# Key parts stored row by row in turn, fewer transfers for queries and gate weights, a three-instruction root refinement and halved low-part subtractions in a two-layer fp32 encoder trunk

## Chip, cores and metric

The kernel runs on one core of one Trainium2 chip, as one launch. The metric is the device time of a run in microseconds (us); lower is better. The kernel before took 2789.21 us (median of three runs, 2776.15 to 2790.53). The engines are called PE (TensorE), DVE (VectorE), ACT (ScalarE), POOL (GpSimd) and SP (SyncE, which here only issues transfers).

## What is computed

Input and output are 2048 tokens of 1024 fp32 features. Layer 0 is a root-mean-square norm, one projection, two attention mixers side by side (A: a sliding window with two key heads for eight query heads, rotary embedding, attention sinks; B: eight heads over the token's own chunk and eight chunks before, with a relative bias), SiLU gates, an output projection and a residual add. Layer 1 has a norm, one projection, differential attention (C) over all earlier chunks, gates, an output projection and a residual add. Cut to what matters:

```python
def rms_norm(x, g):
    y = x * lax.rsqrt(jnp.mean(x * x, axis=-1, keepdims=True) + EPS)
    return y * g

def odd_layer(x, ...):
    h = rms_norm(x, norm_g)
    q, k, v, gate = jnp.split(h @ w_in, [C_QK, 2 * C_QK, 2 * C_QK + C_W], axis=-1)
    q1, q2 = (apply_rope(t, cos, sin) for t in parts(rms_norm(q, qn)))   # two 64-wide parts a head
    k1, k2 = (apply_rope(t, cos, sin) for t in parts(rms_norm(k, kn)))
    lam = exp(sum(lq1 * lk1)) - exp(sum(lq2 * lk2)) + lambda_init
    a = softmax(mask(q1 @ k1.T / 8)) - lam * softmax(mask(q2 @ k2.T / 8))
    o = rms_norm(a @ v, subln_g) * (1.0 - lambda_init)
    return x + (o * silu(gate)) @ w_out
```

## The kernel before, in words

The kernel is written in a tile language whose compiler pass allocates buffers, sets the semaphores and orders the instructions of each engine by a simulated timeline. The order in which the program traces its work is thus a priority and not the order on an engine; `issue_after(ins)` binds the instructions in its block to come behind `ins` on the same engine.

Nearly all products are taken at reduced precision in three passes: each operand is split into a high part (rounded by an ACT copy) and a low part (operand minus high part), and `mm3` (L211 to L216) multiplies high by high, high by low and low by high. So weights, hidden states, queries and keys exist as two tensors each, named H and L.

Four stages follow each other, with overlaps. The projection of layer 0 (`_project`, from 0 to about 600 us) and that of layer 1 (about 1090 to 1720 us) run over column groups of the weights and, within a group, over two blocks of 512 tokens, in two halves. `hidden` (L314) loads four x tiles of 128 tokens, takes the sum of squares on ACT, the inverse root in `rstd` (L196), scales the tile by root and gain on DVE (L325), transposes it on PE (L330) and splits it (L334 on ACT, L335 on DVE). `weights_by` (L298) loads two row blocks of 512 columns at a time and splits them: high part on ACT (L307), low part on POOL (L309), except four tiles of the very first group on DVE. A query or key group then has, for each 128 tokens, its sum of squares (L358, L359), its root in `rstd`, a scaling on DVE (L369), rotary products on DVE and POOL (L375 to L381), transposes (L388), and its split parts are stored to HBM by SP (L398, L399). `rstd` takes a first value y0 = exp(-0.5 ln(scale * ss + eps)) on ACT (L203, L204) and refines it by one Newton step in four DVE instructions (L205 to L208); the first of them does not read y0.

The mixers of layer 0 (`_mix0`, about 600 to 1090 us) and of layer 1 (`_mix1`, about 1720 to 2785 us) load queries and keys back from HBM, head by head. Scores need the query's high part against the key's high and low parts stacked on 128 partitions: 64 rows of high part, 64 rows of low part. So a key tile is filled by two transfers of 64 partitions (L591 and L592 in layer 0's `load_k`; L1104 and L1105 in layer 1's), and each query part is written twice into one tile, once for each half (L581 to L585; L937). In layer 1 an exponential (L969) follows each block of scores; DVE first takes the row maximum (L966). `combine` scales and adds the two softmaxes (L1001 on ACT, L1002 and L1003 on POOL); `values` transposes them on PE (L1017, into a PSUM pool `ptr` of two buffers), copies them on DVE (L1019) and multiplies by the values (L1021).

When a head's output is complete, `gate` copies it from PSUM and traces, two key tiles later, `rest` (L1053): the mean of squares as a product with ones on PE (L1056, into a buffer of the same pool `ptr`), its logarithm on ACT (L1057), a sum on DVE, an exponential on ACT (L1059), a product on DVE (L1060). The gates of layer 1 are projected beside the attention (`gates`, L1153): their split weights come from HBM in pieces of four row blocks, high and low part by one transfer each (L1165). The output projection of layer 1 fetches finished heads back (`fetch`, L1092), splits them on ACT and POOL (L1082, L1083), and runs on PE as `com`.

SP issues nearly all transfers from one in-order queue; each takes it about 0.3 to 0.6 us, and an issue that waits for a buffer holds up all behind it.

Of the kernel before, what the change touches and what calls it, by code (L numbers as in the profile page):

```python
# [18 lines left out]
P = 128  # L19
# [67 lines left out]
class Trunk:  # L87
# [15 lines left out]
    def scratch(self):  # L103
        dram = self.ctx.enter_context(self.tc.tile_pool(name="scr", bufs=1, space=DRAM))

        def d(name, shape):
            return dram.tile(shape, F32, tag=name, name=name)

        self.s0 = {
            "aqH": d("aqH", [4, P, S]), "aqL": d("aqL", [4, P, S]),  # L110
            "akH": d("akH", [1, P, S]), "akL": d("akL", [1, P, S]),
            "av": d("av", [S, 2 * 192]),
            "bqH": d("bqH", [4, P, S]), "bqL": d("bqL", [4, P, S]),
            "bkH": d("bkH", [4, P, S]), "bkL": d("bkL", [4, P, S]),
# [5 lines left out]
            "qH": d("qH", [8, P, S]), "qL": d("qL", [8, P, S]),  # L120
            "kH": d("kH", [8, P, S]), "kL": d("kL", [8, P, S]),
# [4 lines left out]
            "wgH": d("wgH", [8, P, KT, P]), "wgL": d("wgL", [8, P, KT, P]),  # L126
# [69 lines left out]
    def rstd(self, pool, ss, n, scale, tag):  # L196
# [5 lines left out]
        ln, y0, ms, u, r = t("ln"), t("y0"), t("ms"), t("u"), t("r")  # L202
        nc.scalar.activation(ln, ss, AF.Ln, bias=self.eps, scale=scale)  # L203
        nc.scalar.activation(y0, ln, AF.Exp, scale=-0.5)  # L204
        nc.vector.tensor_scalar(ms, ss, scale, EPS, ALU.mult, ALU.add)  # L205
        nc.vector.scalar_tensor_tensor(u, y0, -0.5, y0, ALU.mult, ALU.mult)
        nc.vector.tensor_tensor(u, u, ms, ALU.mult)
# [16 lines left out]
    def _project(self, es, layer):  # L224
# [35 lines left out]

        g_in = xp.tile([P, D], F32, tag="g_in", name=n + "g_in", bufs=1)
# [36 lines left out]
        def weights_by(c0, width, W, wH, wL, first=False):  # L298
            for kh in range(4):
# [5 lines left out]
                for k in range(2):  # L305
                    h, l = weight_tiles()
                    nc.scalar.activation(h[:, :width], ws[:, k, :width], AF.Copy)  # L307
                    low = nc.vector if first and k else nc.gpsimd
                    low.tensor_tensor(l[:, :width], ws[:, k, :width], f32(h[:, :width]), ALU.subtract)  # L309
                    wH.append(h)  # L310
                    wL.append(l)
                yield

        def hidden(b, i, between=()):  # L314
            hH, hL = hidden_tile("H", i), hidden_tile("L", i)
            between = iter(between)
            for j in range(NTB):
                t = b * NTB + j
                xt = xp.tile([P, D], F32, tag="xt", name=n + "xt")
                nc.sync.dma_start(xt, x[t * P:(t + 1) * P, :])  # L320
# [4 lines left out]
                nc.vector.scalar_tensor_tensor(xt, xt, r, g_in, ALU.mult, ALU.mult)  # L325
# [58 lines left out]
        def pairs_out(xs, npair, b, o):  # L384
            for p in range(npair):
# [12 lines left out]
                nc.sync.dma_start(s[o["dH"]][o["p0"] + p, :, b * BLK:(b + 1) * BLK], f32(eH))  # L398
                nc.sync.dma_start(s[o["dL"]][o["p0"] + p, :, b * BLK:(b + 1) * BLK], f32(eL))  # L399
# [9 lines left out]
        def put_gate(s, i, k, part, w):  # L409
            nc.sync.dma_start(  # L410
                s["wg" + part][4 * i:4 * i + 4, :, k, :].rearrange("c p d -> p c d"), w.rearrange("p (c d) -> p c d", c=4)
# [20 lines left out]
        for half in range(2):  # L432
# [4 lines left out]
            if half == 0 and layer == 0:  # L437
# [3 lines left out]
                h = [hidden(blocks[0], 0, by)]  # L441
# [111 lines left out]
    def _mix0(self, es):  # L553
# [22 lines left out]
        def load_q(H, L, h, b, res):  # L576
# [4 lines left out]
            nc.sync.dma_start(f32(qd[0:HD, :]), s[H][h // 2, r, tok])  # L581
            nc.sync.dma_start(f32(qd[HD:P, :]), s[H][h // 2, r, tok])
            ql = ld.tile([P, BLK], F32R, tag="ql", name=n + "ql", bufs=3)
            nc.sync.dma_start(f32(ql[0:HD, :]), s[L][h // 2, r, tok])
            self.asked = nc.sync.dma_start(f32(ql[HD:P, :]), s[L][h // 2, r, tok]).ins  # L585
            res["q"] = (qd, ql)

        def load_k(ks, H, L, p, row, k0, k1):
# [21 lines left out]
        def load_group(b, g):  # L610
# [3 lines left out]
            load_k(ks, "akH", "akL", 0, g, k0, k1)  # L614
# [114 lines left out]
        def scores_b(h, b, res):  # L729
            k0, k1 = max(0, (b - 1) * BLK), (b + 1) * BLK  # L730
            load_q("bqH", "bqL", h, b, res)
            ks = load_k(ld.tile([P, 1024], F32R, tag="ks", name=n + "ks"), "bkH", "bkL", h // 2, h % 2, k0, k1)
# [171 lines left out]
    def _mix1(self, es):  # L904
# [25 lines left out]
        def load_q(h, b):  # L930
            tok = slice(b * BLK, (b + 1) * BLK)
            qd = ld.tile([P, 2, BLK], F32R, tag="qd", name=n + "qd")
            ql = ld.tile([P, 2, BLK], F32R, tag="ql", name=n + "ql")
            for part, q in (("qH", qd), ("qL", ql)):
                both = s[part][h, :, tok].rearrange("(m r) t -> r m t", m=2)
                for o in range(2):
                    nc.sync.dma_start(f32(q[o * HD:(o + 1) * HD]), both)  # L937
# [103 lines left out]
        def gate(h, b, O, g):  # L1041
# [11 lines left out]
            def rest():  # L1053
# [3 lines left out]
                nc.scalar.activation(sq, ms, AF.Ln, bias=self.eps, scale=1.0 / P)  # L1057
# [16 lines left out]
        def y_tiles(h, b):  # L1074
# [3 lines left out]
            return [pl.tile([P, BLK], F32R, tag=t, name=n + "y" + t, bufs=3 if pl is ld else None) for t in tags]  # L1078
# [296 lines left out]
```

## Time and profile before

| | us | share of the span |
|---|---|---|
| profiled execution | 2787.15 | |
| its span | 2785.3 | |
| PE busy | 2684.9 | 96% |
| PE weight loads (beside PE) | 2162.2 | 78% |
| DVE busy | 1815.7 | 65% |
| ACT busy | 1594.9 | 57% |
| POOL busy | 1412.4 | 51% |

The granted PE clock is 0.994 of full speed on average. The transfers of the SP and ACT queues take 61.9% of the time of the 16 DMA engines, 518.50 MB in all.

In the rows that follow, a line of the waits names the engine and source line, the instruction that it waited for, and then us in total, times and longest. A line of the time-ordered view gives start, duration, engine, line, operation, output<-inputs, shape and count; in brackets the idle time before it and what ended it. Names are those of tiles, with a letter or two ahead for the stage (p0 and p1: projections, m: mixers of layer 0, c: mixer of layer 1).

### The profile page before, as it was taken

The page shows a single profiled execution, that of the slowest core. Times are in us where ns is not written, and L with a number is a line of the kernel's source. Part 1 is how long each engine was busy: PE and PEld are TensorE (multiplying, and loading weights), DVE is VectorE, ACT ScalarE, POOL GpSimd, SP SyncE. Part 2 cuts the span into 40 slices and gives each one's busy share as a digit, 9 for nine tenths or more (in the row PEclk, how much of TensorE's full clock was granted, in tenths as well). Part 3 has the DMA queues.
Part 4 walks back from the last instruction along what each step waited for, and adds up shares of the span by engine and source line. Part 5 has one row for each costly group of instructions (what it writes and reads, how often), then busy time and mean ns, then how long its engine had stood idle before and what let it go on. Part 6 is the DMA issues. An engine that isn't in the chain of part 4 may idle for free.

```text
span 2785.3 us, 43597 instructions
## 1 busy us (share of the span) xinstructions
PE 2684.9 (96%) x13384; PEld 2162.2 (78%) x13384; DVE 1815.7 (65%) x4520; ACT 1594.9 (57%) x3975; POOL 1412.4 (51%) x1471
## 2 busy tenths in 40 slices
PE   7999999999899999999999999999999999999999
PEld 5888887888788888788887888777777776676776
DVE  7762286337777777447833783478887777776762
ACT  5443544358767676333343333588887776676771
POOL 3641254245435344336453652467775666667661
PEclk9999999999999999999999999999999999999999
DMA  5674348569787766744494436899877766465542
GB/s 173 226 241 146 110 131 274 189 180 242 203 217 180 185 186 194 218 167 129 143 291 164 144 122 211 249 243 244 212 218 206 198 183 188 121 185 145 166 127 93
DMA packets 350585, 518.50 MB, mean 186 GB/s; under 512 B 42384, under 2 KB 134288, under 8 KB 350352
## 3 DMA queue, kind: packets, MB, share of 16 engines
q1 hardware_dynamic: 345744, 507.32, 61.9%
q10 hardware_dynamic: 4608, 8.39, 0.8%
q8 instruction: 107, 1.75, 0.3%
q14 instruction: 126, 1.03, 0.1%
HBM read 358.56 MB, written 157.02 MB: 185 GB/s over the span
## 4 chain that ended last, share of the span: by engine, by line
PE 69%; DMA 5%; DVE 4%; ACT 3%; issue 1%; POOL 1%; SPq 0%; ACTq 0%; DVEq 0%; POOLq 0%
PE cO L1021 7%; PE p1mm L214 6%; PE p1mm L215 6%; PE p1mm L216 6%; PE cS L962 4%; PE cS L963 4%; PE ctr L1017 3%; PE mom L214 2%; PE mom L216 2%; PE mom L215 2%; PE mtrB L782 2%; PE com L214 2%; PE com L216 2%; PE com L215 2%; PE cG L214 2%; PE cG L215 2%
## 5 line engine op out<-in xcount | busy, mean ns | idle before, releaser
L969 ACT ACTIVATE cP<-cS,cnm 128x512 f32<-128x512 f32 (+3 forms) x640 | 394.6, 623 | 148.9 <-DVE cnm L966 132.6
L966 DVE TENSOR_REDUCE cnm<-cS 128x1 f32<-128x512 f32 (+3 forms) x640 | 373.7, 601 | 55.1 <-PE cS L963 48.7
L1003 POOL TENSOR_TENSOR cP<-cP,cP 128x512 f32<-128x512 f32 (+1 forms) x320 | 357.3, 1144 | 19.0 <-ACT cP L1001 18.6
L1002 POOL TENSOR_SCALAR cP<-cP,crl,cel 128x512 f32<-128x512 f32 (+3 forms) x288 | 208.4, 736 | 261.5 <-DVE crl L984 126.3
L309 POOL TENSOR_TENSOR p0wL<-p0ws,p0wH 128x512 fp32r<-128x512 f32 (+1 forms) x140 | 169.8, 1238 | 279.2 <-ACT p0wH L307 261.3
L214 PE MATMUL p1mm<-p1wH,p1hH 128*128 128x512 f32 x768 | 300.7, 393 | 0.8 <-ACT p1hH L334 0.8
L216 PE MATMUL p1mm<-p1wH,p1hL 128*128 128x512 f32 x768 | 300.2, 391 | 0.0
L215 PE MATMUL p1mm<-p1wL,p1hH 128*128 128x512 f32 x768 | 299.5, 390 | 0.0
L1021 PE MATMUL cO<-cpt,cv 128*128 128x512 f32 (+3 forms) x640 | 285.5, 531 | 9.1 <-DVE cpt L1019 9.0
L962 PE MATMUL cS<-ck,cqd 128*128 128x512 f32 (+3 forms) x640 | 261.7, 413 | 11.6 <-ACT cP L969 10.3
L1019 DVE COPY cpt<-ctr 128x512 f32<-128x512 f32 (+1 forms) x320 | 190.7, 605 | 101.7 <-PE ctr L1017 98.8
L214 PE MATMUL p0mm<-p0wH,p0hH 128*128 128x512 f32 (+1 forms) x640 | 238.0, 375 | 6.9 <-ACT p0vt L497 5.0
L216 PE MATMUL p0mm<-p0wH,p0hL 128*128 128x512 f32 (+1 forms) x640 | 238.9, 374 | 1.6 <-DVE p0hL L335 1.6
L215 PE MATMUL p0mm<-p0wL,p0hH 128*128 128x512 f32 (+1 forms) x640 | 239.1, 374 | 0.0
L963 PE MATMUL cS<-ck,cql 128*128 128x512 f32 (+3 forms) x640 | 234.0, 370 | 1.4 <-DMA cql<-qL 1.4
L1017 PEld LDWEIGHTS ctr<-ident,cP 128*128 128x128 f32 x1088 | 136.8, 141 | 119.4 <-issue 62.6
L309 POOL TENSOR_TENSOR p1wL<-p1ws,p1wH 128x512 fp32r<-128x512 f32 x112 | 152.3, 1383 | 134.2 <-ACT p1wH L307 129.4
L1001 ACT ACTIVATE cP<-cP,cc 128x512 f32<-128x512 f32 (+1 forms) x320 | 189.0, 653 | 16.4 <-DVE cc L987 15.4
L1017 PE MATMUL ctr<-ident,cP 128*128 128x128 f32 x1088 | 174.4, 273 | 5.7 <-POOL cP L1003 5.7
L214 PEld LDWEIGHTS p1mm<-p1wH,p1hH 128*128 128x128 f32 x768 | 144.6, 188 | 29.8 <-ACT p1hH L334 1.2
L216 PEld LDWEIGHTS p1mm<-p1wH,p1hL 128*128 128x128 f32 x768 | 144.3, 188 | 29.7
L767 POOL TENSOR_SCALAR mPB<-mPB,mbr 128x640 f32<-128x640 f32 (+4 forms) x128 | 92.5, 735 | 147.6 <-DVE mbr L764 89.6
(320 smaller groups left out, 6972.9 us busy)
## 6 DMA issues: line engine op xcount, KB each, us to landing
p1ws<-in_od_w_in_dram SPq DMA_DIRECT2D x56, 512.0 KB, 3.7
p0ws<-in_ev_w_in_dram SPq DMA_DIRECT2D x48, 512.0 KB, 4.6
ck<-kH SPq DMA_DIRECT2D x144, 128.0 KB, 3.8
ck<-kL SPq DMA_DIRECT2D x144, 128.0 KB, 3.9
cv<-v SPq DMA_DIRECT2D x72, 256.0 KB, 4.6
cqd<-qH SPq DMA_DIRECT2D x64, 256.0 KB, 6.5
cql<-qL SPq DMA_DIRECT2D x64, 256.0 KB, 7.8
cwH<-wgH SPq DMA_DIRECT2D x64, 256.0 KB, 5.5
```

Source lines behind the costliest of these rows:

```text
L214: mm(ps, aH, bH, start=first, stop=False)
L215: mm(ps, aH, bL, start=False, stop=False)
L216: mm(ps, aL, bH, start=False, stop=last)
L309: low.tensor_tensor(l[:, :width], ws[:, k, :width], f32(h[:, :width]), ALU.subtract)
L962: mm(ps, qd[:, m, js], kt[:, :wd], start=True, stop=False)
L963: self.anchor = mm(ps, ql[:, m, js], kt[:, :wd], start=False, stop=True).ins
L966: nc.vector.tensor_reduce(nm[:, m, z:z + 1], ps, AX.X, ALU.max, negate=True)
L969: exp = nc.scalar.activation(chunks[z][:, :wd], ps, AF.Exp, bias=nm[:, m, z:z + 1], accum_out=acc).ins
L1002: nc.gpsimd.tensor_scalar(p1, p1, rl[:, 0:1], e1, ALU.mult, ALU.mult)
L1003: nc.gpsimd.tensor_tensor(p1, p1, p2, ALU.add)
L1017: nc.tensor.transpose(turned[:, (j - j0) * P:(j - j0 + 1) * P], us[j][kt // 4][:, kk:kk + P], self.ident)
L1021: mm(O[:, j0 * P:], v, T[:, :wd], start=(kt == 0), stop=(kt == nkt - 1), skip_group_check=True)
```

## The change

Seven things are changed.

1. Keys: high and low parts lie in one HBM tensor, `[pairs, 128, 2, 2048]`, so that row r's high part is followed by its low part. A key tile is then loaded by one transfer of 128 partitions, whose partition 2r + i holds part i of row r. The stores of the projections write every other 8 KB row of this tensor.
2. Queries: the doubled query is loaded with one transfer for each part, each row read twice into neighbouring partitions. In layer 1 the HBM tensor becomes `[8, 64, 4, 2, 512]`, so that one row of one block is 4 KB in one piece; a query store of layer 1's projection becomes two transfers of 64 partitions.
3. Gate weights of layer 1: high and low part in one HBM tensor and one SBUF tile, one transfer where there were two.
4. `rstd`: three DVE instructions behind y0 instead of one ahead and three behind.
5. The first x tile of layer 0 is loaded ahead of the gain, and its scaling is done in two halves of 512 columns.
6. The low parts of the weights in layer 0 are subtracted in two halves of 256 columns (layer 1 keeps one instruction).
7. In `rest`, the logarithm is bound to come behind the latest exponential of the scores (`self.exp`) on ACT.

The diff, cut to its core:

```diff
@@ scratch
+        ak, bk, ck = d("ak", [1, P, 2, S]), d("bk", [4, P, 2, S]), d("ck", [8, P, 2, S])
...
-            "qH": d("qH", [8, P, S]), "qL": d("qL", [8, P, S]),
-            "kH": d("kH", [8, P, S]), "kL": d("kL", [8, P, S]),
+            "qH": d("qH", [8, HD, NB, 2, BLK]), "qL": d("qL", [8, HD, NB, 2, BLK]),
+            "k": ck, "kH": ck[:, :, 0], "kL": ck[:, :, 1],
...
-            "wgH": d("wgH", [8, P, KT, P]), "wgL": d("wgL", [8, P, KT, P]),
+            "wg": d("wg", [8, P, 2, KT, P]),
@@ rstd
-        nc.vector.tensor_scalar(ms, ss, scale, EPS, ALU.mult, ALU.add)
-        nc.vector.scalar_tensor_tensor(u, y0, -0.5, y0, ALU.mult, ALU.mult)
-        nc.vector.tensor_tensor(u, u, ms, ALU.mult)
+        nc.vector.scalar_tensor_tensor(u, ss, EPS / scale, y0, ALU.add, ALU.mult)
+        nc.vector.scalar_tensor_tensor(u, u, -0.5 * scale, y0, ALU.mult, ALU.mult)
         nc.vector.scalar_tensor_tensor(r, u, 1.5, y0, ALU.add, ALU.mult)
@@ _project
+        early = load_x((NB - 1) * NTB) if layer == 0 else None
         g_in = xp.tile([P, D], F32, tag="g_in", name=n + "g_in", bufs=1)
...
-                    low.tensor_tensor(l[:, :width], ws[:, k, :width], f32(h[:, :width]), ALU.subtract)
+                    step = width // 2 if layer == 0 and width == 512 else width
+                    for c in range(0, width, step):
+                        cs = slice(c, c + step)
+                        low.tensor_tensor(l[:, cs], ws[:, k, cs], f32(h[:, cs]), ALU.subtract)
...
-                nc.vector.scalar_tensor_tensor(xt, xt, r, g_in, ALU.mult, ALU.mult)
+                step = 512 if first else D
+                for c in range(0, D, step):
+                    cs = slice(c, c + step)
+                    nc.vector.scalar_tensor_tensor(xt[:, cs], xt[:, cs], r, g_in[:, cs], ALU.mult, ALU.mult)
...
-                nc.sync.dma_start(s[o["dH"]][o["p0"] + p, :, b * BLK:(b + 1) * BLK], f32(eH))
-                nc.sync.dma_start(s[o["dL"]][o["p0"] + p, :, b * BLK:(b + 1) * BLK], f32(eL))
+                for part, t in (o["dH"], eH), (o["dL"], eL):
+                    to = s[part][o["p0"] + p]
+                    if layer == 0 or o["tab"] == "k":
+                        nc.sync.dma_start(to[:, b * BLK:(b + 1) * BLK], f32(t))
+                        continue
+                    for m in range(2):
+                        nc.sync.dma_start(to[:, b, m], f32(t[m * HD:(m + 1) * HD]))
@@ _mix0
+            for q, part in (qd, H), (ql, L):
+                twice = s[part][h // 2, r, tok].unsqueeze(1).to_broadcast([HD, 2, BLK])
+                self.asked = nc.sync.dma_start(f32(q), twice).ins
...
-            nc.sync.dma_start(f32(ks[0:HD, :k1 - k0]), s[H][p, r, k0:k1])
-            nc.sync.dma_start(f32(ks[HD:P, :k1 - k0]), s[L][p, r, k0:k1])
+            nc.sync.dma_start(f32(ks[:, :k1 - k0]), s[K][p, r, :, k0:k1].rearrange("r i t -> (r i) t"))
@@ _mix1
-                both = s[part][h, :, tok].rearrange("(m r) t -> r m t", m=2)
-                for o in range(2):
-                    nc.sync.dma_start(f32(q[o * HD:(o + 1) * HD]), both)
+                twice = s[part][h, :, b].rearrange("r m t -> r (m t)").unsqueeze(1).to_broadcast([HD, 2, 2 * BLK])
+                nc.sync.dma_start(f32(q).rearrange("p m t -> p (m t)"), twice)
...
-                nc.scalar.activation(sq, ms, AF.Ln, bias=self.eps, scale=1.0 / P)
+                with tc.issue_after(self.exp):
+                    nc.scalar.activation(sq, ms, AF.Ln, bias=self.eps, scale=1.0 / P)
...
-            nc.sync.dma_start(f32(k[r, :]), s["kH"][h, r, tok])
-            self.loaded = nc.sync.dma_start(f32(k[o, :]), s["kL"][h, r, tok]).ins
+            rows = s["k"][h, m * HD:(m + 1) * HD, :, tok].rearrange("r i t -> (r i) t")
+            self.loaded = nc.sync.dma_start(f32(k), rows).ins
...
-                            for part in "HL":
-                                t = ld.tile([P, 4, P], F32R, tag="w" + part, name=n + "w" + part, bufs=3)
-                                self.loaded = nc.sync.dma_start(f32(t), s["wg" + part][c, :, k:k + 4, :]).ins
+                            w = ld.tile([P, 2, 4, P], F32R, tag="w", name=n + "w", bufs=3)
+                            self.loaded = nc.sync.dma_start(f32(w), s["wg"][c, :, :, k:k + 4, :]).ins
```

More of the change, by code (lines that the diff above doesn't have):

```diff
@@ L259, in weight_tiles, with load_x @@
                     yield self.yt.tile([P, 512], F32R, tag="yt", name=n + "w" + part)
+        def load_x(t):
+            xt = xp.tile([P, D], F32, tag="xt", name=n + "xt")
+            nc.sync.dma_start(xt, x[t * P:(t + 1) * P, :])
+            return xt
+        early = load_x((NB - 1) * NTB) if layer == 0 else None
         g_in = xp.tile([P, D], F32, tag="g_in", name=n + "g_in", bufs=1)
@@ L318, in hidden @@
                 t = b * NTB + j
-                xt = xp.tile([P, D], F32, tag="xt", name=n + "xt")
-                nc.sync.dma_start(xt, x[t * P:(t + 1) * P, :])
+                first = early is not None and j == 0
+                xt = early if first else load_x(t)
                 junk = xp.tile([P, D], F32, tag="vb", name=n + "junk", bufs=2 - layer)
@@ L410, in put_gate @@
             nc.sync.dma_start(
-                s["wg" + part][4 * i:4 * i + 4, :, k, :].rearrange("c p d -> p c d"), w.rearrange("p (c d) -> p c d", c=4)
+                s["wg"][4 * i:4 * i + 4, :, "HL".index(part), k, :].rearrange("c p d -> p c d"),
+                w.rearrange("p (c d) -> p c d", c=4),
             )
@@ L440, in _project @@
                 next(by)
-                h = [hidden(blocks[0], 0, by)]
+                h = [hidden(blocks[0], 0, by, early)]
             else:
@@ L731, in scores_b @@
             load_q("bqH", "bqL", h, b, res)
-            ks = load_k(ld.tile([P, 1024], F32R, tag="ks", name=n + "ks"), "bkH", "bkL", h // 2, h % 2, k0, k1)
+            ks = load_k(ld.tile([P, 1024], F32R, tag="ks", name=n + "ks"), "bk", h // 2, h % 2, k0, k1)
             vt = lv.tile([P, 8, P], F32R, tag="v", name=n + "vB")
@@ L930, in load_q @@
         def load_q(h, b):
-            tok = slice(b * BLK, (b + 1) * BLK)
             qd = ld.tile([P, 2, BLK], F32R, tag="qd", name=n + "qd")
@@ L1077, in y_tiles @@
             pl, tags = place[h, b]
-            return [pl.tile([P, BLK], F32R, tag=t, name=n + "y" + t, bufs=3 if pl is ld else None) for t in tags]
+            if pl is ld:
+                t = ld.tile([P, 2, BLK], F32R, tag="w", name=n + "yw", bufs=3)
+                return t[:, 0, :], t[:, 1, :]
+            return [pl.tile([P, BLK], F32R, tag=t, name=n + "y" + t) for t in tags]
         def split(h, b, o):
@@ L1139, in _mix1 @@
         ended = set()
-        place = {(h, NB - 1): (ld, ("wH", "wL")) if h < 3 else (kp, ("k0", "k1")) for h in (0, 1, 2, 6, 7)}
+        place = {(h, NB - 1): (ld, None) if h < 3 else (kp, ("k0", "k1")) for h in (0, 1, 2, 6, 7)}
         def load_w(c, k, to):
```

21 lines of the change are left out of this document (7 added, 14 removed).

## The prediction

> **What bounds the kernel now.** I read the engine shares on the page first, then what TensorE (PE) waits for, then the windows table, then time-ordered rows around the longest waits.
>
> ```profile
> span 2785.3 us, 43597 instructions
> ...
> PE 2684.9 (96%) x13384; PEld 2162.2 (78%) x13384; DVE 1815.7 (65%) x4520; ACT 1594.9 (57%) x3975; POOL 1412.4 (51%) x1471
> ...
> L969 ACT ACTIVATE cP<-cS,cnm 128x512 f32<-128x512 f32 (+3 forms) x640 | 394.6, 623 | 148.9 <-DVE cnm L966 132.6
> ```
>
> TensorE is busy 96% of the span, and the change touches none of its matmuls. So all that can be won lies in its idle time, 2785.3 - 2684.9 = 100.4 us, and in time that it runs at a reduced clock. The profiled execution took 2787.15 us, 1.85 us more than its span; the median of the three runs is 2789.21 us (2776.15 to 2790.53). I work out a difference against the profiled execution and take it off the median. Of this kernel a measurement can tell about 0.5%, 14 us, from no change.
>
> What PE waits for (engine and line, releaser: us in total, times, longest):
>
> ```profile
> PE p0trh L330 <- DVE p0xt L325: 13.4, 3, 12.7
> PE cS L962 <- ACT cP L969: 10.3, 9, 4.1
> ...
> PE cG L214 <- DMA cwH<-wgH: 5.2, 3, 4.3
> PE p0mm L214 <- ACT p0vt L497: 5.0, 4, 2.3
> ...
> PE p0trq L388 <- DVE p0xn L369: 2.1, 1, 2.1
> PE mSB L626 <- DMA mql<-bqL: 2.1, 1, 2.1
> PE cS L963 <- DMA cql<-qL: 1.4, 3, 0.7
> ```
>
> The idle time is many short waits with different releasers; no single one is worth 14 us. The windows show where they lie, and a second cost behind them (stretch and length; busy time of each engine; granted PE clock, DMA share, GB/s):
>
> ```profile
> 0.00:70.00 70.00, 51.83 (x243) 41.99 (x244) 55.40 (x127) 36.05 (x85) 23.43 (x24) 0.98 0.56 174
> 420.00:490.00 70.00, 66.92 (x309) 54.86 (x308) 42.98 (x96) 32.07 (x78) 32.31 (x31) 0.98 0.83 276
> 1400.00:1470.00 70.00, 67.41 (x333) 55.99 (x331) 27.24 (x46) 35.19 (x70) 36.57 (x28) 1.00 0.95 308
> 1540.00:1610.00 70.00, 70.00 (x334) 58.47 (x333) 56.62 (x87) 22.96 (x47) 44.15 (x34) 1.00 0.40 125
> 1750.00:1820.00 70.00, 65.68 (x295) 51.44 (x296) 32.73 (x115) 39.40 (x105) 29.60 (x35) 0.95 0.86 254
> 1890.00:1960.00 70.00, 67.96 (x332) 51.17 (x331) 61.82 (x196) 62.65 (x174) 52.45 (x60) 1.00 0.99 247
> ```
>
> Where PE stalls for more than about 2 us, the granted clock of the window falls too: 0.95 of 70 us is 3.5 us lost on top of the wait, 0.98 is 1.4. In layer 1's projection (1540 to 1610) PE is busy all 70.00 us: nothing can be won there, and added work on other engines costs nothing.
>
> **The change, part by part.**
>
> *The start.* The first x tile goes ahead of the gain, and its scaling is cut in two.
>
> ```profile
> 0.73 0.38 SPq L262 DMA_DIRECT2D p0g_in<-in_ev_norm_dram  x1
> 1.17 0.42 SPq L301 DMA_DIRECT2D p0ws<-in_ev_w_in_dram  x1
> 1.64 0.46 SPq L320 DMA_DIRECT2D p0xt<-in_x_dram  x1
> ...
> 18.62 1.15 ACT L307 ACTIVATE p0wH<-p0ws 128x512 fp32r<-128x512 f32 x2 [1.72 <-DMA p0ws<-in_ev_w_in_dram]
> ```
>
> PE's first transposes wait 12.7 us. With x as the first of three 512 KB transfers instead of the third, and half a scaling ahead of them, they can begin up to some 5 us sooner. But the first output tile sums over all eight row blocks of the weights, and the last two are converted at 18.62 us, after a transfer whose place in the queue the change leaves alone. So most of the lead is given back there. I take -2 us, bounds -5 and +1 (the first weights are now third in line).
>
> *Low parts in halves, and the root in three.* The 128x512 subtractions of layer 0 on POOL become two of 128x256. Rows of DVE, of POOL, and durations by line (ns min/median/max):
>
> ```profile
> 462.72 1.22 DVE L207 TENSOR_TENSOR p0q8u<-p0q8u,p0q8ms 128x8 f32<-128x8 f32 x1
> 463.98 1.19 DVE L208 SCALAR_TENSOR_TENSOR p0q8r<-p0q8u,p0q8y 128x8 f32<-128x8 f32 x1
> ```
> ```profile
> 461.37 5.00 POOL L309 TENSOR_TENSOR p0wL<-p0ws,p0wH 128x512 fp32r<-128x512 f32 x4 [9.44 <-ACT p0wH L307]
> ```
> ```profile
> L309 POOL TENSOR_TENSOR p0wL<-p0ws,p0wH x140: 723/1290/1485, 7.3 to 600.2; 128x512 fp32r<-128x512 f32 x124, 128x256 fp32r<-128x256 f32 x16
> ```
> ```profile
> L205 DVE TENSOR_SCALAR p0q8ms<-p0qss x48: 160/172/1256, 35.1 to 515.7; 128x8 f32<-128x8 f32 x48
> ```
> ```profile
> 2357.12 2.62 DVE L980 TENSOR_TENSOR cbelow<-cnm,ctop 128x8 f32<-128x8 f32 x1
> ```
>
> A DVE instruction on 128x8 takes 0.17 us as a rule and 1.2 here. POOL's four run 1.25 us each, so they end at 462.62, 463.87, 465.12; the two DVE instructions end at 463.94 and 465.17, each just behind one. So DVE is held to the end of POOL's instruction, and three dependent ones take three of them, 3.75 us. The smallest form, 0.72 us, must be the 256-wide one, so the hold falls to 3 x 0.72 = 2.2, 1.5 less. The trace charges PE with 2.1 us for the wait behind this chain (L388), and with 5.0 for four behind L497, which copies the tiles that the same kind of chain scales; the longest is 2.3. Taking 1.5 off the 2.1, 1.5 off the 2.3 and 1.0 off the other three, with the 1.4 of reduced clock in 420 to 490, gives -5 us. POOL's price, 124 x (2 x 0.72 - 1.29) = 19 us, is covered where POOL is busy for 32 of 70 us; uncovered it is what the rotated tiles queue behind, 1 to 2 us. Bounds -7 and +2.
>
> The Trainium skill, SBUF — State Buffer, section "SBUF: two separate sides", says that POOL and DVE share a pair of ports, locked for the whole instruction by whoever starts first. The rows above agree; by that rule POOL's second half may also start first, and L980 above, which sat through more than one POOL instruction, shows that this happens. Then the part is worth nothing; it counts in the second case below.
>
> The root refinement drops L205: 128 calls by the code (80 in layer 0, 48 in layer 1) x 0.17 = 22 us of DVE. The dropped instruction did not depend on the root's first value; three dependent ones stay behind that. So -1 us, bounds -3 and 0.
>
> *Fewer transfers.* A key load goes from two DMAs of 64 partitions to one of 128, a query from four to two, a gate weight from two to one. SP's queue, ACT, and the issues (KB each, median us to landing):
>
> ```profile
> 2558.96 0.60 SPq L937 DMA_DIRECT2D cql<-qL  x1
> 2559.67 0.54 SPq L1092 DMA_DIRECT2D coy<-o  x1
> ```
> ```profile
> 2567.98 0.63 ACT L1082 ACTIVATE cy<-coy 128x512 fp32r<-128x512 f32 x1 [4.18 <-DMA coy<-o]
> ```
> ```profile
> ck<-kL SPq DMA_DIRECT2D x144, 128.0 KB, 3.9
> cv<-v SPq DMA_DIRECT2D x72, 256.0 KB, 4.6
> cqd<-qH SPq DMA_DIRECT2D x64, 256.0 KB, 6.5
> ...
> qH<-p1eH SPq DMA_DIRECT2D x32, 256.0 KB, 2.8
> ```
>
> A transfer of 256 KB by 64 partitions lands in 6.5 us, one by 128 in 4.6. Where half-height loads prevail (1890 to 1960) the DMA engines move 247 GB/s at a share of 0.99, in the window at 1400 308 at 0.95: 249 against 324 for a full share. I take that ratio, 0.77, for the backlog. In the rows above a fetch queued behind queries was issued at 2559.67 and used at 2567.98, 8.3 us later; ACT stood still for 4.18 us with exponentials behind it, and PE waited 4.1 (the longest of cS <- ACT). A backlog shorter by 0.23 x 8.3 = 1.9 us takes 1.9 off this wait, 1.9 off the query wait of 2.1, 2.8 off the three gate-weight waits (4.3 to 2.4, the short ones to nothing) and 1.4 off L963: 8.0. Of the reduced clock behind these (3.5 in 1750 to 1820, where the gate weights' wait lies, and by estimate a 0.98 window's 1.4 behind each of the other two long ones, 6.3 in all), I let a third go with them, 2 us. So -10 us; bounds 0 (same bytes, same time) and -19 (all of 12.8 us of waits and of 6.3 of clock).
>
> The Trainium skill, SBUF — State Buffer, section "Door 1: The DMA port swizzle", holds that 64 adjacent partitions reach half of the ports. By that rule alone half-height loads take double time, and this part would be near its -19. The trace's ratio is 0.77, not 0.5, and I keep to it.
>
> In return each query store in layer 1's projection becomes two of 64 partitions: 64 more issues by 0.6 us, 38 us of SP there, and some transfer time on a DMA share of 0.40. PE has no idle time to lose to it in that stage, its weights being loaded ahead. 0 us; 3 if the cover goes.
>
> *The logarithm behind the exponential (L1057).*
>
> ```profile
> ACT csq L1057 <- PE cms L1056: 42.9, 12, 10.9
> ```
>
> ACT stands still 42.9 us in twelve places of 32 (8 heads x 4 blocks) because the logarithm is queued ahead of exponentials whose inputs are there, and waits for a product that PE reaches later. Tied behind the latest exponential, it waits little. Most of ACT's idle time is covered: of the 10.3 us of cS <- ACT, 4.1 is the fetch above, and 6.2 are left for this and all else. I take half, -3, bounds -6 and a loss, below.
>
> The sum: -2 - 5 - 1 - 10 + 0 - 3 = -21 us, 2787.15 to 2766 in the profiled frame, 2768 us as a median. The ends add to -40 and, without the loss below, to +6.
>
> **The rivals.**
>
> *Waits move and nothing is seen.* The same bytes cross the same 16 engines, so landings hardly improve; POOL's second half starts before DVE gets in; an earlier start is eaten by later weights. Then the start gives 1 to 2, the root 1, the logarithm 3: 2789 - 6 = 2783 us. For it: DMA waits are only 10 of 100 us of PE's idle time, and the order of instructions on all engines is laid out anew, so other short waits can appear. Against it: the ratio 0.77, and a hold that ends with each POOL instruction.
>
> *Slower: the logarithm holds a PSUM buffer.* Its input, the mean of squares, lies in one of only two buffers that PE also transposes into. Behind an exponential that itself waits for DVE's maximum (132.6 us of such waits in the row of L969), the logarithm frees that buffer later, and PE has one left for transposes. If each of the 32 is later by two exponentials of 0.62 us and PE has nothing else, that is +40 us; with 18 us of other gains, 2789 + 22 = 2811 us. It decides from 1 us each (32 us, less 18, is 14). For it: twenty of the 32 show no wait today, so they can only get later. Against it: PE's queue holds output products and scores for such gaps, and the exponential's scores stand ahead of the mean in PE's queue, so it should rarely be late.
>
> *The change does not do what it says.* One DMA with rows in turn might run as slowly as two; that is in the first rival.
>
> **How the numbers follow.** Forecast, 2768 us: 0.57, its own range 2752 to 2779. No change, 2783: 0.32. Slower, 2811: 0.11. The forecast's range straddles 2775, where faster by over 0.5% begins, and a little of the second case falls below it: faster 0.54, same 0.37, slower 0.09. The range goes from 2752, just above the low end of the terms (2789 - 40), to 2793, which takes in the second case with a few us of new waits and leaves out the third: 0.8 of the chance.
>
> **What would show it.** Right: the cwH, mql and coy waits shorter by about 2 us each and the DMA share at 1890 to 1960 well under 0.99 at like GB/s; DVE's small instructions in 350 to 490 at 0.7 us instead of 1.2 beside POOL, and L497's and L388's waits nearly gone; a granted clock of 1.00 at 420 to 490 and above 0.95 at 1750; ACT's wait at L1057 under 15 us; PE's first transposes near 8 us but the same stage's end only 2 us earlier. Wrong: landings of the merged loads as long as now; PE waiting for the logarithm through its transposes (ctr); new waits of several us in layer 0's projection behind POOL; or the stages already full, 1190 to 1680, growing longer.

## The result and the profile after

The kernel after takes 2770.66 us (median of 7 runs, 2766.57 to 2773.44), the kernel before 2789.21 (median of 7, 2776.15 to 2793.66): a ratio of 0.9949 [0.993, 0.9969]. The forecast was 2768. Beside the experiments the kernel before was timed again, with medians of 2784.83 (35 runs), 2783.23 (14) and 2782.72 (29); against these the gain is 12 to 14 us, not 18.5. The kernel after was timed only here, beside the 2789.21, and not again with them. So a difference of a few us between its 2770.66 and the kernels of the experiments is uncertain; the firmer comparisons are those among kernels timed together. Profile against profile the gain is 16.0 us (2787.15 to 2771.11). The page of after:

```profile
span 2769.3 us, 43201 instructions
...
PE 2681.2 (97%) x13384; PEld 2159.7 (78%) x13384; DVE 1768.0 (64%) x4397; ACT 1595.9 (58%) x3975; POOL 1438.4 (52%) x1595
...
L984 ACT ACTIVATE cP<-cS,cnm 128x512 f32<-128x512 f32 (+3 forms) x640 | 395.4, 624 | 144.6 <-DVE cnm L981 131.8
```

PE's idle time falls from 100.4 us to 2769.3 - 2681.2 = 88.1, and its busy time, with the same 13384 matmuls, by 3.7 us: less of it at a reduced clock. The two make the 16.0. Where they lie is read from the windows by stage, before and after (stretch and length, busy time and count of each engine, granted PE clock, DMA share, GB/s):

```profile
0.00:600.00 600.00, 571.82 (x2825) 479.37 (x2826) 319.05 (x691) 266.73 (x604) 229.44 (x225) 0.99 0.57 186
600.00:1115.00 515.00, 491.75 (x3090) 431.36 (x3089) 382.69 (x1284) 376.76 (x1001) 243.07 (x333) 1.00 0.75 200
1115.00:1720.00 605.00, 599.10 (x2829) 499.06 (x2828) 359.24 (x594) 205.87 (x416) 279.21 (x210) 1.00 0.54 175
1720.00:2785.30 1065.30, 1022.24 (x4646) 752.37 (x4644) 754.68 (x1952) 745.49 (x1954) 660.70 (x704) 0.99 0.66 186
```
```profile
0.00:600.00 600.00, 574.32 (x2836) 480.72 (x2837) 286.96 (x616) 267.19 (x605) 253.74 (x351) 0.99 0.56 186
600.00:1115.00 515.00, 492.92 (x3090) 432.13 (x3089) 382.98 (x1280) 377.50 (x1002) 242.02 (x331) 0.99 0.66 199
1115.00:1720.00 605.00, 597.20 (x2815) 497.07 (x2814) 345.06 (x549) 205.14 (x416) 280.32 (x210) 1.00 0.58 177
1720.00:2769.30 1049.30, 1016.75 (x4649) 749.75 (x4647) 753.05 (x1952) 746.07 (x1954) 662.37 (x704) 1.00 0.59 188
```

In the last stage, layer 1's mixer, PE's idle time goes from 43.1 to 32.6 us: 10.5 of the 12.3 us. The first two stages give 2.5 and 1.2, and the third takes 1.9 back, at its start: between 1115 and 1190 us all thirteen kernels other than the one before, the one with the logarithm alone among them, lose 1.2 to 3.7 us to it, so this is no single part's price. PE's waits after, the lines that answer to those of before:

```profile
PE p0trh L343 <- DVE p0xt L338: 9.6, 2, 7.5
...
PE cS L977 <- ACT cP L984: 5.4, 9, 1.5
PE p0mm L215 <- ACT p0wH L314: 4.5, 1, 4.5
...
PE p0mm L215 <- ACT p0vt L516: 3.9, 3, 1.6
...
PE p0trq L401 <- POOL p0xn L394: 2.3, 2, 1.2
PE p0trq L401 <- DVE p0xn L382: 2.3, 2, 1.2
...
PE mSB L643 <- DMA mql<-bqL: 0.8, 1, 0.8
PE cG L215 <- DMA cw<-wg: 0.8, 1, 0.8
```

The waits for transfers shrink: gate weights from 5.2 to 0.8, layer 0's query from 2.1 to 0.8, layer 1's query (1.4) is gone, and PE's longest wait for an exponential, which stood behind a late fetch, goes from 4.1 to 1.5. (ACT's own wait for that fetch does not shrink; more on it below.) New is the `p0mm` line behind `p0wH`, 4.5 us for the first weights: most of what the early start won. The windows that the prediction showed:

```profile
420.00:490.00 70.00, 67.38 (x319) 55.52 (x320) 37.13 (x83) 33.52 (x79) 39.53 (x60) 1.00 0.84 284
1540.00:1610.00 70.00, 70.00 (x334) 58.48 (x333) 50.41 (x79) 23.10 (x48) 43.86 (x33) 1.00 0.53 133
1750.00:1820.00 70.00, 69.22 (x322) 54.26 (x321) 34.44 (x124) 41.05 (x107) 33.57 (x39) 1.00 0.87 278
1890.00:1960.00 70.00, 68.46 (x326) 50.58 (x324) 59.13 (x191) 63.03 (x173) 53.13 (x61) 1.00 0.81 256
```

At 1750 PE is busy 3.5 us longer at full clock. At 1890 the DMA engines move 256 GB/s at a share of 0.81, where they moved 247 at 0.99: 316 against 249 for a full share. Landings after (KB each, median us), and ACT's wait before the logarithm:

```profile
ck<-ck SPq DMA_DIRECT2D x144, 256.0 KB, 4.6
cw<-wg SPq DMA_DIRECT2D x64, 512.0 KB, 5.3
...
cqd<-qH SPq DMA_DIRECT2D x32, 512.0 KB, 6.5
cql<-qL SPq DMA_DIRECT2D x32, 512.0 KB, 7.2
```
```profile
ACT csq L1073 <- PE cms L1071: 34.2, 11, 10.9
```

A merged query transfer lands about as late as one of the two did (6.5 and 7.2 against 6.5 and 7.8), with twice the bytes; a merged key transfer takes 4.6 us against 3.8 and 3.9.

### The profile page after: what moved, and what is told of

It reads as the page before. It is cut to its first block, busy times and chain, and to the rows that moved or that the text cites. A ratio compares the mean times of both kernels' runs of the same rounds, so it can differ in the third digit from the quotient of the medians.

```text
span 2769.3 us, 43201 instructions
## 1 busy us (share of the span) xinstructions
PE 2681.2 (97%) x13384; PEld 2159.7 (78%) x13384; DVE 1768.0 (64%) x4397; ACT 1595.9 (58%) x3975; POOL 1438.4 (52%) x1595
## 4 chain that ended last, share of the span: by engine, by line
PE 80%; DVE 5%; ACT 4%; DMA 3%; issue 2%; POOL 1%; SPq 0%; ACTq 0%; DVEq 0%; POOLq 0%
PE cO L1036 8%; PE p1mm L215 6%; PE p1mm L216 6%; PE p1mm L217 6%; PE cS L977 4%; PE cS L978 4%; PE ctr L1032 4%; PE p0mm L217 3%; PE p0mm L216 3%; PE p0mm L215 3%; PE mom L215 2%; PE mom L217 2%; PE mom L216 2%; PE cG L215 2%; PE cG L216 2%; PE cG L217 2%
## 5 line engine op out<-in xcount | busy, mean ns | idle before, releaser
L1018 POOL TENSOR_TENSOR cP<-cP,cP 128x512 f32<-128x512 f32 (+1 forms) x320 | 356.8, 1142 | 18.4 <-ACT cP L1016 18.3
L319 POOL TENSOR_TENSOR p0wL<-p0ws,p0wH 128x256 fp32r<-128x256 f32 x264 | 192.6, 765 | 268.9 <-ACT p0wH L314 255.4
```

What stands on the lines that cost most here:

```text
L319: low.tensor_tensor(l[:, cs], ws[:, k, cs], f32(h[:, cs]), ALU.subtract)
L1018: nc.gpsimd.tensor_tensor(p1, p1, p2, ALU.add)
```

## The experiments

Theory at the start: fewer and whole-height transfers make most of the gain, the parts of layer 0 and the logarithm the rest. Rivals: the parts of layer 0 alone; the order of work laid out anew; the number of transfers rather than their shape. All ratios are against the kernel before, timed beside each kernel. The four runs of the first two headings ("one part at a time" and "the gate weights") are one set, the four on the logarithm, layer 0's parts and the keys another, and the last four a third. A lead is how many us earlier PE starts the same product than in the profile of the kernel before.

**One part at a time.** Parts 1 to 3 of the change alone, in the kernel before:

```diff
+            rows = s["k"][h, m * HD:(m + 1) * HD, :, tok].rearrange("r i t -> (r i) t")
...
+                twice = s[part][h, :, b].rearrange("r m t -> r (m t)").unsqueeze(1).to_broadcast([HD, 2, 2 * BLK])
...
+                            w = ld.tile([P, 2, 4, P], F32R, tag="w", name=n + "w", bufs=3)
```

> The kernel before with the merged key, query and gate-weight transfers alone (parts 1 to 3 of the change); root, start, halves and logarithm as before. Theory T, fewer and full-height transfers bring the gain: 2771 to 2776 us, nearly all of the change's 18.5 us, won behind 1750 us of the span; gate-weight wait under 1.5 us, clock at 1750 to 1820 back to 1.00. Theory L, the logarithm's place brings it: 2785 us or more. Theory S, a newly laid-out order of instructions shifts the time by some us whatever is changed: anything between 2775 and 2795, with new waits elsewhere.

Measured: 2777.55 us (2770.57 to 2788.13, 12 runs), 0.9976 [0.9959, 0.9993]: a gain, but 1.6 us short of theory T's range. Its profile still has a gate-weight wait of 2.2 us and a clock of 0.98 at 1750 to 1820; that execution, 2785.3 us, was its second slowest.

Part 7 alone:

```diff
+                with tc.issue_after(self.exp):
+                    nc.scalar.activation(sq, ms, AF.Ln, bias=self.eps, scale=1.0 / P)
```

> The kernel before with only the logarithm bound behind the latest exponential (part 7). Theory T: 2784 to 2789 us, 0 to 5 us faster. Theory L: 2771 to 2778 us. Both: ACT's idle time ahead of the logarithm falls from 42.9 us to between 30 and 37, since the changed kernel still has 34.2. Theory S: 2775 to 2795 us.

Measured: 2785.72 us (2781.76 to 2795.4, 12 runs), 1.0011 [0.9997, 1.0025]. ACT's idle time ahead of the logarithm, expected at 30 to 37 us, was 46.7: it did not fall.

Parts 4 to 6 alone:

```diff
+        early = load_x((NB - 1) * NTB) if layer == 0 else None
...
+                    step = width // 2 if layer == 0 and width == 512 else width
```

> The kernel before with the early x tile, the halves and the three-instruction root alone (parts 4 to 6). The changed kernel is only 2.2 us ahead at the end of layer 0's projection, against 7 to 8 that my sum had for these parts. If that is what they are worth: 2785 to 2789 us. If they are worth 7 to 8 us and the merged transfers took some back in layer 0: 2781 to 2783 us. First transposes at about 7.5 us of the span in either case.

Measured: 2783.05 us (2775.68 to 2788.53, 12 runs), 1.0003 [0.9988, 1.0017], on the edge of the second range. Its one profile shows a span of 2776.6 us, under this median: a single profile says where time lies, not how much a kernel is worth.

Alone, only the transfers are worth something, 7.3 us of medians. The three sum to about 8 us and the whole change gave 12 to 14; the intervals leave it open whether that difference is real.

**The gate weights.** After with part 3 undone:

```diff
+                            for part in "HL":
+                                t = ld.tile([P, 4, P], F32R, tag="w" + part, name=n + "w" + part, bufs=3)
+                                self.loaded = nc.sync.dma_start(f32(t), s["wg" + part][c, :, k:k + 4, :]).ins
```

> The changed kernel with high and low gate weights in two tensors, tiles and transfers again (part 3 undone). The changed kernel gained 6.0 us between 1751 and 1787 of the span, where PE had waited 4.3 us for gate weights at a clock of 0.95. If the merged gate weights bring that: 2776 to 2779 us, with that wait back. If the shorter key and query transfers ahead of them in the queue bring it: 2770 to 2773 us, no such wait.

Measured: 2770.66 us (2767.09 to 2778.99, 12 runs), 0.9961 [0.9947, 0.9974]: their merge is worth nothing that shows. The rows of its DMA issues say why:

```profile
cwH<-wgH SPq DMA_DIRECT2D x64, 256.0 KB, 4.5
...
cwL<-wgL SPq DMA_DIRECT2D x64, 256.0 KB, 4.9
```

These transfers are those of the kernel before, where they landed in 5.5 and 5.7 us. Where keys and queries have their old loads they take 5.4 to 6.0 us (the logarithm alone, layer 0's parts alone), so it is the new key and query loads that bring them in sooner. Which of the two is not shown: merged gate weights land in 5.3 us in the kernel after and, below, in 5.3 with queries in halves and 5.5 with keys in halves.

**The logarithm and the parts of layer 0, taken out of the whole.**

```diff
-                with tc.issue_after(self.exp):
-                    nc.scalar.activation(sq, ms, AF.Ln, bias=self.eps, scale=1.0 / P)
+                nc.scalar.activation(sq, ms, AF.Ln, bias=self.eps, scale=1.0 / P)
```

> The kernel after with part 7 undone: the logarithm keeps its old place on ACT. Theory A: the new place of the logarithm lays out PE's order in layer 1's mixer anew, and this order pays only when the loads are in time; alone (old loads) it gave nothing, 2785.72 against 2784.83. Then without it the kernel falls back to what the transfers alone give, 2777.5 us (2774 to 2781). Theory B: the parts of layer 0 are what was missing, and the logarithm is worth nothing with any loads: 2771 us. ACT's wait for the mean of squares: 40 to 50 us under both.

Measured: 2772.87 us (2768.3 to 2774.64, 5 runs), 0.9957 [0.9944, 0.9971].

```diff
+        nc.vector.tensor_scalar(ms, ss, scale, EPS, ALU.mult, ALU.add)
...
-        early = load_x((NB - 1) * NTB) if layer == 0 else None
+        early = None
...
-                    step = width // 2 if layer == 0 and width == 512 else width
+                    step = width
```

> The kernel after with parts 4, 5 and 6 undone (the root in four instructions, the gain first, whole subtractions in layer 0); transfers and logarithm are those of the kernel after. Theory A (transfers and logarithm together make the gain): 2772 us (2769 to 2774), lead over the kernel before near zero up to 600 us and 13 to 15 us at the end. Theory B (the parts of layer 0 add to the transfers, the logarithm adds nothing): 2777 us.

Measured: 2776.5 us (2769.53 to 2779.98, 7 runs), 0.9972 [0.9959, 0.9985]. So theory A, transfers and logarithm together, does not stand, and theory B is the nearer one. But the traces correct both. First, the logarithm does do something, in one stretch; the window 2000 to 2210 of the kernel without it, then of the kernel after:

```profile
2000.00:2210.00 210.00, 204.99 (x932) 149.73 (x930) 164.72 (x422) 164.79 (x435) 139.70 (x149) 0.99 0.65 203
```
```profile
2000.00:2210.00 210.00, 206.94 (x950) 151.52 (x949) 166.44 (x428) 169.38 (x443) 142.32 (x153) 1.00 0.66 207
```

PE's busy time here is 203.66 to 204.99 in all four kernels with the old logarithm and 205.85 to 206.94 in all ten with the new one, whatever the loads: 2 us. It does not come from a shorter wait of ACT, as the prediction had it: ACT waits 2.6 to 2.7 us at the logarithm in this stretch in the kernel before, the one without it and the kernel after alike. What goes is a wait of PE's transposes for POOL (`cP`) of 1.9 us, at 2163 us in the kernel before; all four kernels with the old place have it, and in the ten with the new one no such wait in this stretch is over 0.94. Why the new place removes it is not shown. Part of the 2 us is lost again later.

Second, what the run without layer 0's parts loses is not lost in layer 0 alone. Behind the same piece of work, PE's lead over the kernel before shrinks from 13.9 to 9.4 us at 2507 to 2561 us, in layer 1's mixer. There stands a DVE instruction on 128x8, mostly of 0.17 us, with POOL's row of four beside it; in the kernel without those parts:

```profile
2502.82 4.47 DVE L996 TENSOR_TENSOR cbelow<-cnm,ctop 128x8 f32<-128x8 f32 x1
```
```profile
2502.29 4.97 POOL L1019 TENSOR_TENSOR cP<-cP,cP 128x512 f32<-128x512 f32 x4
```

and in the kernel after:

```profile
2501.60 0.80 DVE L995 TENSOR_TENSOR cbelow<-cnm,ctop 128x8 f32<-128x8 f32 x1
```
```profile
2501.10 4.99 POOL L1018 TENSOR_TENSOR cP<-cP,cP 128x512 f32<-128x512 f32 x4
```

Both start 0.5 us into a row of four. One gets in when the first of the four ends (2501.10 + 1.25 = 2502.35, against 2501.60 + 0.80 = 2502.40), the other only when all four have ended (2507.26 against 2507.29), and PE's output products then wait behind the copies queued on DVE (2.84 us at 2508.54). The kernel with the transfers alone has the same hold (4.51 us) and loses 5.8 us of lead there. Every kernel here has between one and five DVE instructions held to over 1.8 us behind 2300 us, at changing places, the kernel before four. That this is what spreads the runs of one kernel over 6 to 22 us is possible but not shown.

**Number of transfers or their shape: keys.** After, with each key load of layer 1 as two transfers, once by neighbouring halves and once by alternate rows:

```diff
+            for o in range(2):
+                self.loaded = nc.sync.dma_start(f32(k[o * HD:(o + 1) * HD]), rows[o * HD:(o + 1) * HD]).ins
```

> The kernel after, but each key load of layer 1's mixer is two transfers again, one into partitions 0 to 63, one into 64 to 127; the layout in memory and the 2 KB pieces are those of the kernel after. Theory H (a transfer into 64 neighbouring partitions runs slower): each lands in 3.8 us as in the kernel before, the DMA share at 1890 to 1960 goes back from 0.81 to over 0.9 at like GB/s, and the time is 2775 us (2773 to 2778). Theory N (what counts is the number of transfers, 144 more issues of 0.55 us on SP): share unchanged at about 0.81, time 2775 us, and the next kernel just the same. Theory Q (key loads don't matter, queries do): 2771 us.

```diff
+            for i in range(2):
+                self.loaded = nc.sync.dma_start(f32(k).rearrange("(r i) t -> i r t", i=2)[i], s["k"][h, m * HD:(m + 1) * HD, i, tok]).ins
```

> As the run before, with the same number of transfers and the same 2 KB pieces, but one transfer fills the even partitions (all high parts) and one the odd ones (all low parts), so that each spreads over all 128. Theory H: landings under 3.3 us, DMA share at 1890 to 1960 about 0.81, time 2771 us (2769 to 2773), that of the kernel after. Theory N: like the run before, 2775 us. Theory Q: 2771 us, and the run before too.

Measured: 2775.97 us (2770.9 to 2780.65, 8 runs), 0.9971 [0.9961, 0.9981], and 2772.74 us (2770.98 to 2777.0, 5 runs), 0.9964 [0.9952, 0.9977]. The issues, halves first:

```profile
ck<-ck SPq DMA_DIRECT2D x288, 128.0 KB, 3.7
```
```profile
ck<-ck SPq DMA_DIRECT2D x288, 128.0 KB, 3.3
```

With the same number of issues, bytes and 2 KB pieces, neighbouring halves land 0.4 us later. But the DMA share at 1890 to 1960 is 0.83 and 0.82: theory H's 0.9 did not come. The key loads are not what filled the DMA engines. Whether their halves cost time stays open. The two medians lie 3.2 us apart and as theory H had them, but their intervals overlap. In its profile the kernel with halves falls from a lead of 8.3 us at 1820 us to 4.5 at 1830, where PE waits for ACT's copy of gates (`cgt`):

```profile
PE cG L215 <- ACT cgt L1190: 3.6, 1, 3.6
```
```profile
1820.31 0.63 ACT L1065 ACTIVATE csg<-cgg 128x512 f32<-128x512 f32 x1 [7.52 <-DMA cgg<-g]
```

That copy stands on ACT behind an instruction that waits 7.52 us for fetched gates. With alternate rows ACT has the same order, the wait for the gates is 5.77 us, and PE's is 1.9; in the kernel after the copy stands ahead, and PE waits 0.3. So the loads and the order of the instructions share this loss.

**The same for the queries.** After, with each query part as two transfers of 64 neighbouring partitions in 4 KB pieces:

```diff
+                for o in range(2):
+                    half = s[part][h, o * HD // 2:(o + 1) * HD // 2, b].rearrange("r m t -> r (m t)")
+                    nc.sync.dma_start(
+                        f32(q[o * HD:(o + 1) * HD]).rearrange("p m t -> p (m t)"),
+                        half.unsqueeze(1).to_broadcast([HD // 2, 2, 2 * BLK]),
+                    )
```

> The kernel after, but each query part of layer 1 is loaded by two transfers, one into partitions 0 to 63 and one into 64 to 127; layout and 4 KB pieces are those of the kernel after. At 1890 to 1960 us the kernel before moved 247 GB/s at a DMA share of 0.99, the kernel after 256 at 0.81, and splitting the key loads hardly changed that (259 at 0.83). Theory W (64 neighbouring partitions make a transfer slow): share back above 0.93 at like GB/s, time 2775 us (2772 to 2778). Theory P (the piece, 2 KB before and 4 KB after, made it slow): share 0.81, time 2771 us.

and after with the old layout in memory, as two transfers of 128 partitions in 2 KB pieces:

```diff
+                for m in range(2):
+                    twice = s[part][h, m * HD:(m + 1) * HD, b * BLK:(b + 1) * BLK].unsqueeze(1).to_broadcast([HD, 2, BLK])
+                    nc.sync.dma_start(f32(q[:, m]), twice)
```

> The kernel after with the old layout of layer 1's queries in memory: a store is again one transfer of 128 partitions, and a query part is loaded by two transfers, one for each of its two 64-wide parts, each of 128 partitions in 2 KB pieces. Four transfers a query, as in the kernel before, but each over all partitions. Theory W: share at 1890 to 1960 about 0.82, DMA share at 1540 to 1610 back from 0.53 to 0.40, time 2771 us or a little less (2767 to 2773). Theory P: share above 0.93, time 2775 us.

Measured: 2778.14 us (2771.83 to 2783.74, 12 runs), 0.9979 [0.9964, 0.9993], and 2771.99 us (2768.2 to 2774.6, 8 runs), 0.9955 [0.9939, 0.9971]. The window at 1890 and the mixer's, of the halves and of the 2 KB pieces, and the mixer's of the kernel after:

```profile
1890.00:1960.00 70.00, 68.40 (x328) 50.80 (x327) 57.76 (x194) 63.00 (x173) 51.43 (x58) 1.00 0.94 263
...
1720.00:2790.00 1070.00, 1024.12 (x4657) 757.35 (x4655) 749.39 (x1952) 746.62 (x1955) 660.95 (x704) 0.98 0.64 186
```
```profile
1890.00:1960.00 70.00, 68.48 (x331) 50.96 (x328) 59.51 (x194) 63.02 (x173) 53.77 (x62) 1.00 0.88 262
...
1720.00:2790.00 1070.00, 1018.76 (x4641) 753.69 (x4640) 750.24 (x1952) 746.13 (x1954) 660.89 (x704) 0.99 0.61 185
```
```profile
1720.00:2790.00 1070.00, 1016.75 (x4649) 749.75 (x4647) 753.05 (x1952) 746.07 (x1954) 662.37 (x704) 1.00 0.58 184
```

For like GB/s the mixer's DMA share is 0.66 before, 0.64 with the queries in halves, 0.61 with whole transfers in 2 KB pieces, 0.58 after. So theory W holds for the queries. Within one set and with four transfers a query in both, halves are 6.2 us slower than whole-height transfers, and eleven of their twelve runs are slower than the slowest of the other eight; against the kernel after it is 7.5 us of medians, as much as the transfers gave alone. In the profile some of this is the wait just shown for the keys: PE waits 3.6 us at the same place, behind a wait of ACT of 6.72 us. The 2 KB pieces, or the layout or the greater number of transfers that goes with them, cost share too (0.88 at 1890 to 1960, between the two theories) but no time that shows. The run in 2 KB pieces has the old stores and a share of 0.41 at 1540 to 1610 (after: 0.53); PE is busy all 70.00 us there either way.

**The halves of the subtraction, and the early x tile.**

```diff
-                    step = width // 2 if layer == 0 and width == 512 else width
+                    step = width
```

> The kernel after with part 6 undone: the low parts of layer 0's weights are subtracted in one instruction of 128x512 again. If the halves carry what the parts of layer 0 are worth (5.8 us in all by the run without them): 2775.5 us (2773 to 2778), the half clock near 466 us back, lead at 601 us lost. If the start or the root carries it: 2771 to 2772 us.

```diff
-        early = load_x((NB - 1) * NTB) if layer == 0 else None
+        early = None
```

> The kernel after with part 5 undone: the gain is loaded ahead of the first x tile, which is scaled in one piece. If the start is worth about what the traces show of it behind the first tiles (lead 5 us at 14 us, 1 at 64 us): 2771.5 us (2770 to 2773). If it carries what the parts of layer 0 are worth: 2776 us.

Measured: 2774.18 us (2768.88 to 2780.91, 12 runs), 0.9968 [0.9954, 0.9981], and 2774.58 us (2767.78 to 2776.96, 10 runs), 0.9959 [0.9943, 0.9975]. Neither is told apart from the kernel after by its time. By the traces the halves are. DVE's chain behind the root without the halves, then POOL's row there, and both in the kernel after:

```profile
464.15 1.22 DVE L208 SCALAR_TENSOR_TENSOR p0q8u<-p0q8u,p0q8y 128x8 f32<-128x8 f32 x1
465.40 1.19 DVE L209 SCALAR_TENSOR_TENSOR p0q8r<-p0q8u,p0q8y 128x8 f32<-128x8 f32 x1
```
```profile
462.82 6.21 POOL L319 TENSOR_TENSOR p0wL<-p0ws,p0wH 128x512 fp32r<-128x512 f32 x5 [9.49 <-ACT p0wH L314]
```
```profile
460.32 0.66 DVE L208 SCALAR_TENSOR_TENSOR p0q8u<-p0q8u,p0q8y 128x8 f32<-128x8 f32 x1
461.01 0.66 DVE L209 SCALAR_TENSOR_TENSOR p0q8r<-p0q8u,p0q8y 128x8 f32<-128x8 f32 x1
```
```profile
458.82 6.99 POOL L319 TENSOR_TENSOR p0wL<-p0ws,p0wH 128x256 fp32r<-128x256 f32 x10 [6.66 <-ACT p0wH L314]
```

POOL's instruction falls from 1.24 to 0.70 us, and DVE's hold from 1.2 to 0.66. Between the 462nd and the 522nd us (of the kernel before) all nine kernels with halves gain 1.2 to 2.8 us on it (the kernel after 2.5); the four without, among them the one of this run, lie between 0.1 us gained and 1.1 lost. So the halves are worth 2 us, clock included. The early tile leads by 4.9 us at PE's first product, and at 201 us the kernels with it lie between 1.0 us ahead and 2.8 behind, those without it between 0.3 ahead and 0.6 behind: it is worth nothing that shows.

## Why the prediction was right

The sum was -21 us; the measured gain is 16.0 in the profiles and 12 to 14 against the larger sets of runs. The number 2768 came nearer than its sum, and that is luck: the median of three runs from which it was taken, 2789.21, lay above the later ones of 2782.72 to 2784.83. What was right is the largest term; of the smaller ones two were too large and one, the logarithm's, had the wrong mechanism. Term by term:

| term | predicted | measured |
|---|---|---|
| start | -2 | 0: lead given back by 201 us |
| low parts in halves | -5 | -2 |
| root in three | -1 | not measured alone |
| fewer transfers | -10 | -7.3 alone; queries in halves cost 6.2 within one set |
| query stores doubled | 0 | 0 (PE busy 70.00 of 70; lead -1.1 at 1190, -0.7 at 1680 us) |
| logarithm | -3 | -2 at 2000 to 2210, not seen in the times |

*The transfers* were the right mechanism at about the right size. The waits named are shorter by 9.7 us (gate weights 4.4, layer 0's query 1.3, layer 1's 1.4, the fetch 2.6) where 8.0 were summed, and the clock at 1750 rose to 1.00. But the fetch's share is no gain. A shorter backlog was to take 1.9 us off the wait behind it. ACT's wait for it grew from 4.18 to 5.84 us, and PE now waits at this place behind a DVE instruction held for 4.04 us:

```profile
2560.14 0.63 ACT L1101 ACTIVATE cy<-coy 128x512 fp32r<-128x512 f32 x1 [5.84 <-DMA coy<-o]
```
```profile
2554.37 4.04 DVE L1002 TENSOR_SCALAR cc<-cel,crl,nlam 128x4 f32<-128x4 f32 x1
```
```profile
2559.05 1.12 PE L1036 MATMUL cO<-cpt,cv 128*128 128x512 f32 x2 [3.82 <-DVE cpt L1034]
```

PE's lead is 13.7 us ahead of this place and 13.6 behind it. That leaves 7.1 us of waits where 6.1 were summed. The ratio of 0.77 was borne out: 249 / 316 = 0.79. What was wrong is the owner. "Half-height loads" were blamed together; by the mixer's DMA share it was the queries' above all (0.64 in halves, against 0.60 with the keys in halves and 0.58 after), by time the keys are not cleared, the gate weights' merge is worth nothing, and beside the height there are the 2 KB pieces, which the prediction did not look at. One of the waits named is not tied to any one load: the gate weights' is back with 3.5 us where queries come in halves, with 4.1 where they come in 2 KB pieces, and with 3.1 where only the early x tile is undone. As a test, "landings of the merged loads as long as now" was ill chosen: they are as long for queries and longer for keys, for twice the bytes.

The Trainium skill, SBUF — State Buffer, section "Door 1: The DMA port swizzle", has 64 neighbouring partitions reach half of the ports. The two key runs agree with it in direction, 3.7 against 3.3 us, and nowhere is there a factor of two in time.

*The halves* failed in the step "taking 1.5 off the 2.1, 1.5 off the 2.3 and 1.0 off the other three". The wait of the 2.1, 2.06 us at 465.94, is gone, but L388's line still reads 2.3, and 2.3 more behind POOL: other short waits took its place. L497's fell from 5.0 to 3.9 and its longest from 2.3 to 1.6. The held instructions became 0.66 us, as reasoned, and the clock of 420 to 490 is 1.00, as forecast.

*The start* failed in "I take -2": PE's first transposes come at 7.51 us as predicted, but of the 5 us then 4.5 go into waiting for the weights at 20.89, and the rest in the tiles after it. That the stage ends 2.2 us earlier looks like the forecast but is no sign of it: the kernel with the gate weights apart, the same up to there, ends it 1.3 us later than the kernel before.

*The logarithm*: "ACT's wait at L1057 under 15 us" was wrong, it is 34.2. Of this 18.3 us lie behind 2650 in three waits, before and after alike, where few exponentials are left to go ahead of it; only the other 24.6 could shrink, and became 15.9. Nor is that fall the new place's doing: the same part is 15.9 to 31.4 us in the ten kernels with the new place and 21.3 to 31.3 in the four with the old. The step that failed is "Tied behind the latest exponential, it waits little".

*The rivals.* "Waits move and nothing is seen" falls with the transfers, though waits did move: behind the early start, the halves and the fetch. "Slower", the logarithm holding the transposing buffer, shows as one wait of PE's transposes for it of 0.7 us (1.1 with the old place, in the kernel without part 7), where 1 us on each of 32 was needed; the logarithm alone came to 1.0011 [0.9997, 1.0025].

The prediction's remark that the clock falls where PE stalls for more than about 2 us holds only at times: in the kernel before the clock falls at a stall of 2.06 us at 466 but not at one of 2.97 us at 2362.

*Left open*: what halves of the keys cost; whether layer 0's parts are worth more in the whole change (5.8 us of medians, from two sets) than alone (1.8), since a hold of DVE in layer 1's mixer, which comes and goes, makes up about 3 us of the first in the profiles (4.5 us of lead lost at that place, against 1.4 in the kernel after); and what decides that hold.

## What to carry to other kernels

When transfers into 64 partitions fill the queue, interleave the rows in memory so that one transfer fills all 128, and find by halving one load at a time which of them fills it. Bytes alone do not tell: here the queries (128 transfers of 256 KB before) raised the DMA share more than the keys (288 of 128 KB). A drop of the DMA share at like GB/s, not a shorter landing, shows that it worked. Even transfers that were not touched can then land sooner, as the gate weights did here. A short two-operand DVE instruction beside a row of POOL instructions can wait for the whole row, so take its cost from the row's length and not from one instruction, and don't read single traces of such a stage to better than the holds in them.

## What was not expected of the hardware

The same DVE instruction, 0.5 us behind the start of a row of four POOL instructions, once got in after the first (0.80 us) and twice only after the fourth (4.47 and 4.51). The Trainium skill, SBUF — State Buffer, section "SBUF: two separate sides", says that whoever starts first holds the shared ports for the whole instruction; all three ends fall on the end of a POOL instruction, which agrees, but who comes next between two of them changed with nothing that these traces show.
